# A hybrid attention and delta-rule block: ScalarE copies a pair's open accumulator into a gate's scratch tile, and the last quarter is summed from two tiles

## The chip, the core and the metric

The kernel runs on one core of one Trainium2 chip. The metric is the device time of one execution in microseconds (us). TensorE (PE) multiplies matrices into PSUM, an accumulator memory of banks; VectorE (DVE) and ScalarE (ACT) work element by element on PSUM and on SBUF, the working memory; GpSimd (POOL) does a few small steps; SyncE (SP) issues the transfers. Each engine has an instruction list of its own, which it runs in order, and waits on semaphores for the others.

## The reference

One layer of a hybrid decoder on 16 meta tokens and 512 sequence tokens (528 columns) with a model width of 1024, in float32. Attention and a chunked gated delta rule run side by side on the same normalised input.

```python
hn = rms_norm(h, norm_w)
proj = hn @ w_in                      # widths 1024: aq ak av az dq dk dv dz ..., ga gd
y_a = (o_a * silu(az)) @ w_branch_attn        # o_a: differential attention of aq, ak, av, 8 heads
qkv = silu(causal_depthwise_conv(concat(dq, dk, dv), conv_w))
...
y_d = (o_d * silu(dz)) @ w_branch_delta       # o_d: gated delta rule in chunks of 64, 8 heads
merged = sigmoid(ga) * y_a + sigmoid(gd) * y_d
h = h + merged @ w_out
return rms_norm(h, final_norm_w)[:, N_META:]
```

What counts here is `proj`: each of its blocks is 128 output features x 528 tokens, summed over 1024 inputs.

## The kernel before

**Precision.** Each float32 operand is split into a high and a low part (`wh`, `wl` for weights, `hnH`, `hnL` for the normalised input), and each product is three matmuls: high by high, low by high, high by low (`PASSES`). ACT casts the high part of a weight, DVE subtracts it to get the low one.

**Pairs.** 17 pairs of blocks (`PAIRS`: `ak`, `dk`, `dv`, `dq` blocks with their neighbour) are computed with a Strassen-Winograd scheme: the two blocks by the two halves of the inputs by the two halves of the tokens (`HALF` = 264) form 2x2 block matrices, and seven half-size products replace eight. Each product is 4 input chunks x 3 passes = 12 matmuls with 264 columns. The weights' sums (`wa` to `wd`) are made on DVE while they are split; the tokens' sums lie in `sumH0..3` and `sumL0..3`. The table gives each product its PSUM accumulator, weight, half and part of the tokens, in the order of execution; in a pair `p4` goes to an accumulator `q` of its own:

```python
PRODUCTS = dict(p1=("r", "wa", 0, "b11"), p2=("s", "wa", 1, "b21"), p6=("r", "wb", 1, "t2"), p5=("t", "wb", 0, "t1"),
                p7=("r", "wc", 0, "t3"), p4=("r", "wc", 1, "t4"), p3=("t", "wd", 0, "b22"))
```

The four quarters of a pair (block m, tokens tau) are sums over the products' running sums:

- block 0, first tokens: `r` after p1 (copied by ACT, `snap`) plus `s`
- block 0, second tokens: `r` after p6 (copied by ACT) plus `t` after p3, which p3 adds to p5
- block 1, first tokens: `r` after p7, copied by ACT into the SBUF tile `cn` (`snap_c`), plus `q` (p4)
- block 1, second tokens: `cn` plus `t` after p5, *before* p3 adds to it

The sums are DVE additions of a bank and an SBUF tile (`total`). The third product, p3, is the last of the seven and adds to `t`; so PE waits ahead of it for the event `c+`, which the DVE addition of the last quarter gives when it has read `t`. The sums go to an `xp` tile for `dk`, `dv`, `dq` (a convolution follows) and to a `vT` tile for `ak`, `av`.

**Order.** The program writes every step as a generator that asks for a slot or an event and then for an engine. A planner (`Plan`, lines 95 to 205) gives each engine its next instruction by the earliest estimated time and a rank. The lists are fixed when the program is built: a step that is added or waits for something else makes the planner deal the rest again. Between the matmuls of pairs and single blocks (`product`) stand small products of attention (`ident,e`, `vm,pmT`, `psc<-ak,aq`) and of the delta rule (`S,kT`, `vin,TM`, `u,ktd`, `TM,tds` and the like).

**Slots.** Three weight slots `W`; accumulators from six PSUM banks, at most three for dense products (`pd`); two scratch tiles of a gate, `th` (the two halves of the tile `room3`, 128x512 each), which hold the tanh of a `dz` or `az` block from its ACT instruction until DVE has used it. They become free when the tokens' sums are made.

All instructions go through one helper, so the profile names line 231 for each; rows are told apart by their tiles.

Of the kernel before, what the change touches and what calls it, by code (L numbers as in the profile page):

```python
# [14 lines left out]
ALU = mybir.AluOpType  # L15
# [18 lines left out]
def dense_order():  # L34

    order = []
    for g in range(H // 2):
        k, v, q, z = ([(n, 2 * g), (n, 2 * g + 1)] for n in ("dk", "dv", "dq", "dz"))
        a0, a1 = ([(n, 2 * g + i) for n in ("ak", "av", "aq", "az")] for i in range(2))
        order += k + v + (a0 + q + a1 + z if g else q + a0[2:3] + z[:1] + a0[:2] + a0[3:] + z[1:] + a1)  # L40
    order += [("gd", c) for c in range(KB)] + [("ga", 0)]
    for n in range(KB):
        order += [("ga", n + 1)] * (n < KB - 1) + [(("yd", "ya")[n // 4], 2 * (n % 4) + i) for i in range(2)]
    return order
# [6 lines left out]
                p7=("r", "wc", 0, "t3"), p4=("r", "wc", 1, "t4"), p3=("t", "wd", 0, "b22"))  # L51
# [6 lines left out]
ORDER = dense_order()  # L58
# [3 lines left out]
HALF = L // 2  # L62
# [6 lines left out]
PE, DVE, ACT, POOL, SP = "PE", "DVE", "ACT", "POOL", "SP"  # L69
# [19 lines left out]
class Plan:  # L89
# [24 lines left out]
    def spawn(self, gen, rank=None):  # L114
        time, src = self.here() if self.task else (0.0, SP)
        self.tasks.append(Task(gen, self.task.rank if rank is None else rank, time, src))

    def done(self, event):
        self.events[event] = self.here()
# [146 lines left out]
def hybrid_block(ctx: ExitStack, tc: tile.TileContext, x, meta, wblk, wbd, wout, pcol, prow, out):  # L266
    nc = tc.nc
    plan = Plan({**SLOTS, "wo": 0, "th": 0}, BANKS, ALL_BANKS)
    T, V, A, G, S = (Engine(plan, n, e) for n, e in
                     ((PE, nc.tensor), (DVE, nc.vector), (ACT, nc.scalar), (POOL, nc.gpsimd), (SP, nc.sync)))  # L270
    spawn, done = plan.spawn, plan.done
# [9 lines left out]
    def mk(pl, shape, dt, tag, bufs=None):  # L281
        uid[0] += 1
        kw = {} if bufs is None else {"bufs": bufs}
        return pl.tile(shape, dt, tag=tag, name=f"{tag}_{uid[0]}", **kw)
# [12 lines left out]
    def bank(kind):  # L297

        return mk(ps, [P, 2, 512], F32, kind, SLOTS[kind]) if kind == "psc" else banks_[plan.task.slot]

    def give(kind, at=None):
        plan.give(kind, names_.index(at.tensor.name) if kind in BANKS else 0)
# [9 lines left out]
    def tick(event, n):  # L312
        ticks[event] = ticks.get(event, 0) + 1
        if ticks[event] == n:
            done(event)
        return ticks[event] == n
# [540 lines left out]
    ths = [room[3][:, n, 0:SEQ] for n in range(SLOTS["th"])]  # L857
# [11 lines left out]
    cn = mk(dp, [P, HALF], F32, "cn")  # L869
# [811 lines left out]
    WHOLE = dict(dk=whole_dk, dv=whole_dv, dq=whole_dq, ak=whole_ak, av=whole_av)  # L1681
# [196 lines left out]
    def pair_of_blocks(n):  # L1878

        (n0, i0), (n1, i1) = ORDER[n], ORDER[n + 1]  # L1880
        kind = "xp" if n0 == n1 else "vT"
        acc, to, which = {}, {}, {}
        tokens = slice(0, HALF), slice(HALF, L)

        def take(m):
            if m in which:
                yield f"to {m} {n}"
                return
            which[m] = None
            if kind == "vT":  # L1890
                yield "ap"
            yield (kind,)
            which[m] = plan.task.slot
            to[m] = xps[which[m]][:, 3:3 + L] if kind == "xp" else late["vT"][which[m]]
            done(f"to {m} {n}")

        def snap(key, m, tau):
            yield from take(m)
            yield ACT
            A.copy(out=to[m][:, tokens[tau]], in_=acc["r"])  # L1900
            done(f"{key} {n}")

        def snap_c():
            yield ("cn",)
            yield ACT
            A.copy(out=cn, in_=acc["r"])
            give("pd", acc["r"])
            done(f"c {n}")

        def total(m, tau, of, key, src=None):  # L1910

            yield f"{key} {n}"
            yield from take(m)
            yield DVE
            dst = to[m][:, tokens[tau]]
            V.tensor_tensor(out=dst, in0=acc[of], in1=dst if src is None else src, op=ALU.add)
            if of != "t" or m == 0:
                give("pd", acc[of])
            if of == "t":
                done(f"{key}+ {n}")  # L1920
            if src is not None and tick(f"cn {n}", 2):
                give("cn")
            if tick(f"block {m} {n}", 2):
                name, i = ORDER[n + m]
                spawn(WHOLE[name](i, which[m]), 1)

        follow = dict(p1=lambda: snap("a", 0, 0), p2=lambda: total(0, 0, "s", "a"), p6=lambda: snap("b", 0, 1), p7=snap_c,
                      p4=lambda: total(1, 0, "q", "c", cn), p3=lambda: total(0, 1, "t", "b"))
        for key, (bk, wt, hf, part) in PAIR_PRODUCTS.items():
            if key in ("p6", "p7"):  # L1930
                yield f"{'a' if key == 'p6' else 'b'} {n}"
            if key == "p4":
                spawn(total(1, 1, "t", "c", cn), -1)
            if key == "p3":
                yield f"c+ {n}"
            yield f"{wt} {n}"
            if part in of_sum:
                yield part
            wh, wl, which_w = pairs[n][wt]
            w = wh[:, 512 * hf:512 * hf + 512], wl[:, 512 * hf:512 * hf + 512]  # L1940
            fresh = bk not in acc
            if fresh:
                yield ("pd",)
            for k in range(KB // 2):
                if part in of_sum:
                    x_ = ts_h[of_sum[part]][:, k], ts_l[of_sum[part]][:, k]
                else:
                    x_ = [hn[j][:, k + KB // 2 * (part[1] == "2"), tokens[part[2] == "2"]] for j in range(2)]
                yield PE
                if fresh and k == 0:  # L1950
                    acc[bk] = bank("pd")[:, 0:HALF]
                for m, (a, b) in enumerate(PASSES):
                    T.matmul(acc[bk], w[a][:, k * P:(k + 1) * P], x_[b], start=fresh and k == 0 and m == 0,
                             stop=k == KB // 2 - 1 and m == 2, skip_group_check=not fresh)
            if key in LAST:
                plan.give("W", which_w)
            if key in follow:
                spawn(follow[key](), -1)
        if n == PAIRS[-1]:
            done("sums free")  # L1960
# [33 lines left out]
    def dense():  # L1994
        yield from first_products()
        for n, (name, i) in list(enumerate(ORDER))[2:]:
            if n in PAIRS:
                yield from pair_of_blocks(n)
            elif n not in PAIRED and name not in ("ga", "yd", "ya"):
                yield from product(n)  # L2000
# [244 lines left out]
```

## Time and profile before

| | us |
|---|---|
| median of 3 runs | 752.92 (752.59 to 752.99) |
| profiled execution, its own time | 751.14 |
| span of the profiled execution, first to last instruction | 749.4 |
| TensorE busy | 735.4 (98%) |
| VectorE busy | 629.4 (84%) |
| ScalarE busy | 516.0 (69%) |
| GpSimd busy | 71.8 (10%) |

The span is cut into 40 slices in the page; TensorE is at nine tenths or more in all but the last, and its granted clock is 0.997 on average. 71% of the chain that ended last is TensorE's. In a row of the timeline the first number is the start in us, the second the length drawn; in brackets stands the engine's idle time before the instruction and what ended it. `PEld` is TensorE's loading of the stationary operand, which overlaps its matmuls. In a group's row, `x17 | 6.4, 377` is the count, the total in us and the mean in ns, and after the second bar stand the idle time before such instructions and what ended it.

### The profile page before, as it was taken

To read this page: it belongs to the slowest core of one execution; us is meant where nothing else is said; L and a number is where in the kernel's file an instruction comes from. 1 tells how busy PE (TensorE), PEld (TensorE's weight loads), DVE (VectorE), ACT (ScalarE), POOL (GpSimd) and SP (SyncE) were. 2 spreads that over 40 slices of the span, in tenths; PEclk is the share of its full clock that TensorE was granted. 3 is DMA by queue.
4 is the path that set the end of the run, shared out by engine and by line. 5 is a ranking of instruction groups with operands and counts; after the bars stand their busy time and mean duration, and the time that the engine had idled before them with its cause. 6 is when DMAs were issued, how large, how long until landed. Compare 5 with 4: busy or idle time off the path is not lost.

```text
span 749.4 us, 14381 instructions
## 1 busy us (share of the span) xinstructions
PE 735.4 (98%) x5299; PEld 668.8 (89%) x5299; DVE 629.4 (84%) x1417; ACT 516.0 (69%) x1381; POOL 71.8 (10%) x86
## 2 busy tenths in 40 slices
PE   9999999999999999999999999999999999999996
PEld 7998988899998899998899989888988998899875
DVE  6999999899899889889989898983679879789453
ACT  6369665979974889985597997577785445546132
POOL 2202001202100301300030210000010000000001
PEclk9999999999999999999999999999999999999999
DMA  8130522215232321334032314531122343133602
GB/s 300 59 114 29 142 62 65 70 62 170 62 122 85 73 71 52 120 100 141 29 72 72 120 56 137 212 71 58 57 66 103 142 143 113 54 108 112 231 5 108
DMA packets 45432, 74.34 MB, mean 99 GB/s; under 512 B 20729, under 2 KB 25893, under 8 KB 45362
## 3 DMA queue, kind: packets, MB, share of 16 engines
q1 hardware_dynamic: 45360, 73.43, 30.8%
q8 instruction: 41, 0.67, 0.4%
q14 instruction: 29, 0.24, 0.1%
q10 hardware_dynamic: 2, 0.00, 0.0%
HBM read 67.06 MB, written 6.36 MB: 98 GB/s over the span
## 4 chain that ended last, share of the span: by engine, by line
PE 71%; ACT 12%; DVE 11%; issue 3%; DMA 2%; SPq 0%; POOL 0%; POOLq 0%; DVEq 0%; ACTq 0%
PE bank L231 68%; DVE wl L231 3%; PE psc L231 2%; ACT wh L231 2%; ACT ak L231 1%; ACT TM L231 1%; DMA raw<-in_wblk_dram 1%; DVE tmps L231 1%; DVE ts L231 1%; DMA xt<-in_x_dram 1%; DVE y L231 1%; DVE raw L231 1%; ACT MT L231 1%; DVE ast L231 1%; ACT vr L231 1%
## 5 line engine op out<-in xcount | busy, mean ns | idle before, releaser
L231 PE MATMUL bank<-hnH,wh 128*128 128x512 f32 (+4 forms) x612 | 218.1, 361 | 2.6 <-DVE vT L231 2.1
L231 PE MATMUL bank<-hnL,wh 128*128 128x512 f32 (+4 forms) x612 | 206.1, 342 | 0.0
L231 PE MATMUL bank<-hnH,wl 128*128 128x512 f32 (+4 forms) x612 | 205.8, 342 | 0.0
L231 ACT CAST wh<-raw 128x1024 fp32r<-128x1024 f32 (+1 forms) x123 | 118.0, 960 | 50.7 <-PE bank L231 45.3
L231 DVE TENSOR_TENSOR wl<-raw,wh 128x1024 fp32r<-128x1024 f32 (+1 forms) x123 | 136.8, 1113 | 16.2 <-ACT wh L231 15.8
L231 PEld LDWEIGHTS bank<-hnH,wh 128*128 128x128 f32 x612 | 114.2, 189 | 16.2 <-DVE vT L231 2.8
L231 PEld LDWEIGHTS bank<-hnH,wl 128*128 128x128 f32 x612 | 113.8, 188 | 13.9
L231 PEld LDWEIGHTS bank<-hnL,wh 128*128 128x128 f32 x612 | 114.2, 189 | 10.0
L231 PE MATMUL bank<-sumH,wh 128*128 128x264 f32 x272 | 82.4, 303 | 0.0
L231 PE MATMUL bank<-sumH,wl 128*128 128x264 f32 x272 | 77.2, 284 | 0.0
L231 PE MATMUL bank<-sumL,wh 128*128 128x264 f32 x272 | 77.1, 283 | 0.0
L231 DVE SCALAR_TENSOR_TENSOR y<-xp,pc,y 128x528 f32<-128x528 f32 (+1 forms) x72 | 54.6, 761 | 0.5 <-ACT y L231 0.3
L231 PEld LDWEIGHTS bank<-sumH,wh 128*128 128x128 f32 x272 | 51.5, 189 | 0.6 <-issue 0.2
L231 PEld LDWEIGHTS bank<-sumL,wh 128*128 128x128 f32 x272 | 51.4, 189 | 0.0
L231 PEld LDWEIGHTS bank<-sumH,wl 128*128 128x128 f32 x272 | 51.1, 188 | 0.0
L231 ACT ACTIVATE e<-psc,ast 128x144 f32<-128x144 f32 (+3 forms) x64 | 34.5, 540 | 12.5 <-DVE ast L231 11.4
L231 PE MATMUL bank<-btH,wh 128*128 128x256 f32 x128 | 36.6, 286 | 1.0 <-ACT sn L231 0.9
L231 ACT CAST wh<-st 128x1024 fp32r<-128x1024 f32 x25 | 26.2, 1047 | 15.9 <-PE bank L231 14.6
L231 PE MATMUL bank<-btH,wl 128*128 128x256 f32 x128 | 36.1, 282 | 0.0
L231 PE MATMUL bank<-btL,wh 128*128 128x256 f32 x128 | 36.1, 282 | 0.0
L231 DVE TENSOR_TENSOR wl<-st,wh 128x1024 fp32r<-128x1024 f32 x25 | 30.7, 1229 | 6.2 <-ACT wh L231 6.2
L231 PE MATMUL psc<-ak,aq 128*128 128x264 f32 (+3 forms) x160 | 29.0, 303 | 0.4 <-ACT e L231 0.4
(381 smaller groups left out, 1723.4 us busy)
## 6 DMA issues: line engine op xcount, KB each, us to landing
raw<-in_wblk_dram SPq DMA_DIRECT2D x96, 512.0 KB, 3.5
raw<-in_wout_dram SPq DMA_DIRECT2D x8, 512.0 KB, 4.9
xt<-in_x_dram SPq DMA_DIRECT2D x4, 512.0 KB, 6.6
TM<-gcd SPq DMA_DIRECT2D x8, 256.0 KB, 5.5
xr<-in_x_dram SPq DMA_DIRECT2D x8, 256.0 KB, 6.3
out_dram<-xr SPq DMA_DIRECT2D x7, 256.0 KB, 2.3
room<-scrm SPq DMA_DIRECT2D x12, 128.0 KB, 3.4
oad<-room SPq DMA_DIRECT2D x6, 256.0 KB, 2.0
```

Of the source, the lines that this page charges most:

```text
L231: return real(*args, **kw)
```

## The change

A new step `snap_t` follows the fifth product: it takes a `th` slot, and ACT copies the accumulator `t` (264 columns) into it. The last quarter of a pair is now made by `both`, from the scratch tile and `cn`, so DVE reads two SBUF tiles there and no bank; it then gives the scratch tile back. The third product waits for the copy (event `t`) and no longer for the addition (`c+`). The other three quarters are summed as before; `finished` is the old ending of `total`.

```diff
+        def snap_t():
+            yield ("th",)
+            which["t"] = plan.task.slot
+            yield ACT
+            A.copy(out=ths[which["t"]][:, 0:HALF], in_=acc["t"])
+            done(f"t {n}")
+
+        def both():
+            yield f"t {n}"
+            yield f"c {n}"
+            yield from take(1)
+            yield DVE
+            V.tensor_tensor(out=to[1][:, tokens[1]], in0=ths[which["t"]][:, 0:HALF], in1=cn, op=ALU.add)
+            plan.give("th", which["t"])
+            if tick(f"cn {n}", 2):
+                give("cn")
+            finished(1)
...
         def total(m, tau, of, key, src=None):
...
-            if of != "t" or m == 0:
-                give("pd", acc[of])
-            if of == "t":
-                done(f"{key}+ {n}")
+            give("pd", acc[of])
...
-        follow = dict(p1=lambda: snap("a", 0, 0), p2=lambda: total(0, 0, "s", "a"), p6=lambda: snap("b", 0, 1), p7=snap_c,
+        follow = dict(p1=lambda: snap("a", 0, 0), p2=lambda: total(0, 0, "s", "a"), p6=lambda: snap("b", 0, 1), p5=snap_t, p7=snap_c,
...
             if key == "p4":
-                spawn(total(1, 1, "t", "c", cn), -1)
+                spawn(both(), -1)
             if key == "p3":
-                yield f"c+ {n}"
+                yield f"t {n}"
```

In the built program ACT has 17 more copies, one for each pair, and DVE as many additions as before. PE's matmuls are the same in number and shape. All engines' lists are as before up to the second pair except for the copies and their neighbours; from the third pair on the planner deals the small products differently.

More of the change, by code (lines that the diff above doesn't have):

```diff
@@ L1908, in snap_c, with finished @@
             done(f"c {n}")
+        def snap_t():
[14 more added lines that the diff above has]
+            finished(1)
+        def finished(m):
+            if tick(f"block {m} {n}", 2):
+                name, i = ORDER[n + m]
+                spawn(WHOLE[name](i, which[m]), 1)
         def total(m, tau, of, key, src=None):
@@ L1916, in total @@
             V.tensor_tensor(out=dst, in0=acc[of], in1=dst if src is None else src, op=ALU.add)
-            if of != "t" or m == 0:
-                give("pd", acc[of])
-            if of == "t":
-                done(f"{key}+ {n}")
+            give("pd", acc[of])
             if src is not None and tick(f"cn {n}", 2):
                 give("cn")
-            if tick(f"block {m} {n}", 2):
-                name, i = ORDER[n + m]
-                spawn(WHOLE[name](i, which[m]), 1)
-        follow = dict(p1=lambda: snap("a", 0, 0), p2=lambda: total(0, 0, "s", "a"), p6=lambda: snap("b", 0, 1), p7=snap_c,
+            finished(m)
+        follow = dict(p1=lambda: snap("a", 0, 0), p2=lambda: total(0, 0, "s", "a"), p6=lambda: snap("b", 0, 1), p5=snap_t, p7=snap_c,
                       p4=lambda: total(1, 0, "q", "c", cn), p3=lambda: total(0, 1, "t", "b"))
```

## The prediction

> **What bounds the kernel now.** I read the page's head first, then the busy time by stretch, then who waited for whom on TensorE, and last the rows around the waits.
>
> ```profile
> span 749.4 us, 14381 instructions
> PE 735.4 (98%) x5299; PEld 668.8 (89%) x5299; DVE 629.4 (84%) x1417; ACT 516.0 (69%) x1381; POOL 71.8 (10%) x86
> ```
>
> TensorE (PE) is the bound: it is busy for 735.4 of 749.4 us. Its work does not change (the same 4707 matmuls as the program writes them), so only the 14 us in which it is idle, and what hides inside its busy time, can be won.
>
> ```profile
> core 0: us, PE busy (x) PEld busy (x) DVE busy (x) ACT busy (x) POOL busy (x), PEclk, DMA share, GB/s
> 32.00:135.00 103.00, 101.16 (x705) 92.96 (x703) 96.67 (x225) 74.32 (x191) 12.91 (x12) 1.00 0.30 86
> 135.00:471.00 336.00, 333.01 (x2663) 310.03 (x2663) 304.54 (x718) 279.43 (x831) 42.40 (x41) 1.00 0.29 89
> 471.00:700.00 229.00, 227.95 (x1519) 202.74 (x1520) 184.35 (x368) 135.10 (x306) 5.34 (x6) 1.00 0.33 108
> 700.00:749.40 49.40, 43.17 (x210) 35.75 (x208) 18.56 (x37) 11.56 (x26) 3.30 (x4) 0.99 0.27 95
> ```
>
> The pairs run from 78 to 472 us. From 135 to 471 us PE stands idle for 2.99 us, from 32 to 135 us for 1.84, and the largest idle time, 6.2 us, lies in the last 49 us, which the change does not touch.
>
> ```profile
> PE bank L231 <- DVE vT L231: 2.1, 3, 0.8
> PE bank L231 <- DVE tdmt L231: 0.9, 1, 0.9
> PE bank L231 <- DVE xp L231: 0.2, 1, 0.2
> PEld bank L231 <- DVE vT L231: 2.8, 3, 1.0
> PEld bank L231 <- DVE xp L231: 0.4, 1, 0.4
> ```
>
> The columns are total us, times, longest. The longest line of PE is a wait for VectorE (DVE) writing `vT`, three times; a fourth time it waits for `xp`. `vT` and `xp` are the two kinds of block tile that a pair fills. The four places:
>
> ```profile
> 110.45 0.28 PE L231 MATMUL bank<-sumH,wl 128*128 128x264 f32 x1
> 111.29 0.39 PE L231 MATMUL bank<-hnH,wh 128*128 128x264 f32 x1 [0.55 <-DVE vT L231]
> 111.52 0.28 PE L231 MATMUL bank<-hnL,wh 128*128 128x264 f32 x1
> ...
> 265.03 0.28 PE L231 MATMUL bank<-sumH,wl 128*128 128x264 f32 x1
> 265.52 0.39 PE L231 MATMUL bank<-hnH,wh 128*128 128x264 f32 x1 [0.20 <-DVE xp L231]
> 265.74 0.28 PE L231 MATMUL bank<-hnL,wh 128*128 128x264 f32 x1
> ...
> 345.48 0.28 PE L231 MATMUL bank<-sumH,wl 128*128 128x264 f32 x1
> 346.51 0.39 PE L231 MATMUL bank<-hnH,wh 128*128 128x264 f32 x1 [0.75 <-DVE vT L231]
> 346.74 0.28 PE L231 MATMUL bank<-hnL,wh 128*128 128x264 f32 x1
> ...
> 469.81 0.28 PE L231 MATMUL bank<-sumL,wh 128*128 128x264 f32 x1
> 469.93 0.28 PE L231 MATMUL bank<-sumH,wl 128*128 128x264 f32 x1
> 471.03 0.39 PE L231 MATMUL bank<-hnH,wh 128*128 128x264 f32 x1 [0.82 <-DVE vT L231]
> 471.26 0.28 PE L231 MATMUL bank<-hnL,wh 128*128 128x264 f32 x1
> ```
>
> At each, the fourth product's last matmul (`sumH,wl`) is followed by the third product's first (`hnH,wh`): the spot where the old code waits for `c+`. What it waits for, at the last place, on ScalarE (ACT) and DVE:
>
> ```profile
> 467.27 1.05 ACT L231 CAST wh<-raw 128x1024 fp32r<-128x1024 f32 x1 [1.49 <-PE bank L231]
> 469.07 0.37 ACT L231 COPY cn<-bank 128x264 f32<-128x264 f32 x1
> 469.32 0.50 ACT L231 ACTIVATE e<-psc,ast 128x272 f32<-128x272 f32 x1
> 469.41 1.23 DVE L231 TENSOR_TENSOR wl<-raw,wh 128x1024 fp32r<-128x1024 f32 x1
> 470.55 0.77 DVE L231 TENSOR_TENSOR vT<-bank,cn 128x264 f32<-128x264 f32 x2
> ```
>
> ACT copies `r` into `cn` at 469.07; DVE then still has a weight split of 1.23 us ahead of the sum, starts the sums at 470.55, and PE goes on at 471.03. So the matmuls wait behind a queue, with only the 12 matmuls of the fourth product as cover.
>
> **The change part by part.** *The wait taken away.* Undisturbed matmuls of this shape start 0.12 us apart (469.81 to 469.93). The four gaps are 0.84, 0.49, 1.03 and 1.10 us, so they hold 0.72 + 0.37 + 0.91 + 0.98 = 2.98 us above that spacing. The bracketed idle times add up to 2.32 only; I take the spacing, since a matmul's drawn length (0.28) overlaps the next ones. After each wait the second matmul starts 0.22 to 0.23 us after the first instead of 0.12: 0.11 + 0.10 + 0.11 + 0.11 = 0.43 us more, which I count too. Together -3.4 us; ends -2.3 and -3.4. The weight-load rows, 2.8 + 0.4 = 3.2, lie between.
>
> [...]
>
> *The wait put in.* The third product now waits for ACT's copy of `t`, which follows the fifth product. Behind that stand the seventh and fourth products, 24 matmuls of 0.12 us = 2.9 us.
>
> ```profile
> L231 ACT COPY cn<-bank 128x264 f32<-128x264 f32 x17 | 6.4, 377 | 2.9 <-PE bank L231 2.7
> L231 DVE TENSOR_TENSOR xp<-bank,cn 128x264 f32<-128x264 f32 x18 | 7.6, 428 | 2.9 <-ACT cn L231 2.2 <-PE bank L231 0.6
> L231 DVE TENSOR_TENSOR room<-room,room 128x256 f32<-128x256 f32 x8 | 3.4, 422 | 0.1
> ```
>
> The copy has the shape of the `cn` copy: 0.377 us, of which 0.25 us until ACT takes the next instruction (469.07 to 469.32). 2.9 us of cover leave 2.5, more than any single ACT instruction above. On the path: 0.
>
> *What stands behind the copy on ACT.* At the second pair, where ACT's list has the copy ahead of the weight cast that the same fifth product releases (the rows are the order; `room` is the scratch, `bank_6` holds `t`, `bank_5` holds `r`), before and now:
>
> ```order
> L231 ACTIVATE e_1356,ast_1354<-psc_1363,ast_1354 128x272
> L231 CAST wh_19_117<-raw_16_114 128x1024
> L231 CAST pm_91_717<-e_1290 128x2x16
> L231 COPY cn_167<-bank_5_82 128x264
> L231 CAST pm_92_718<-e_1355 128x2x16
> ```
>
> ```order
> L231 ACTIVATE e_1357,ast_1355<-psc_1364,ast_1355 128x272
> L231 COPY room_33_133<-bank_6_83 128x264
> L231 CAST wh_19_117<-raw_16_114 128x1024
> L231 COPY cn_167<-bank_5_82 128x264
> L231 CAST pm_91_717<-e_1291 128x2x16
> ```
>
> The cast moves 0.25 us back and the `cn` copy moves ahead of a small cast. At the last place of before that cast ran at 467.27 and its split ended at 470.64 (469.41 + 1.23); without the wait the third product would run from 470.05 to 471.5, and only then is the next block needed, so 0.86 us are left and 0.25 fit: 0. If that cover were gone at every pair, 17 x 0.25 = 4.3 us.
>
> *The sum's other source.* DVE reads two SBUF tiles instead of a bank and a tile. The nearest rows are 422 ns for two SBUF tiles with 256 elements and 428 ns with 264 and a bank: the same to 6 ns, 17 x 0.006 = 0.1 us, off PE's path. 0.
>
> *The scratch tiles.* The copy holds one of two, which the gates use too. The row `ACTIVATE room<-bank` shows how little the gates ask of them:
>
> ```profile
> L231 ACT ACTIVATE room<-bank 128x512 f32<-128x512 f32 x18 | 10.8, 599 | 0.2 <-PE bank L231 0.2
> ```
>
> 18 gates in the whole span, and 0.2 us idle before them. 0; at worst a pair waits for one gate's 0.6 us, and that is inside the 2.5 us.
>
> *The new deal.* The planner deals all the work again, and from the third pair on the small products of the chunked delta rule stand elsewhere between the pairs' matmuls. PE at the third pair, around the third product's first rows (`bank_5` holds `t`; `TM,tds` are 32x32 products of the delta rule's inverse), before and now:
>
> ```order
> L231 MATMUL bank_6_83<-tds_1624,TM_744 32x32
> L231 MATMUL bank_6_83<-TM_744,tds_1624 32x32 x8
> L231 MATMUL bank_5_82<-hnH,wh_23_121 128x264
> L231 MATMUL bank_5_82<-hnL,wh_23_121 128x264
> L231 MATMUL bank_5_82<-hnH,wl_24_122 128x264
> ```
>
> ```order
> L231 MATMUL bank_1_78<-vs_1193,pT_1689 128x128 x4
> L231 MATMUL bank_2_79<-sumH_36_136,wh_21_119 128x264
> L231 MATMUL bank_2_79<-sumL_40_140,wh_21_119 128x264
> L231 MATMUL bank_2_79<-sumH_36_136,wl_22_120 128x264
> L231 MATMUL bank_5_82<-hnH,wh_23_121 128x264
> L231 MATMUL bank_5_82<-hnL,wh_23_121 128x264
> L231 MATMUL bank_5_82<-hnH,wl_24_122 128x264
> ```
>
> The small products, which filled the old wait here, now come after the third product and six matmuls of the next block. Everything behind that point is dealt anew, so its waits on chains of small steps are new too, and no row of before shows them. The bounds: PE's idle time from 135 to 471 us outside the waits counted above is 2.99 - 0.20 - 0.75 - 0.82 = 1.22 us, so the gain ends at -1.2. For the loss I take the stretch with the most: from 32 to 135 us it is 1.84 - 0.55 = 1.29 us in 103, which over 336 us would be 4.2, or 3.0 more than now. From 471 to 700 us it is 1.05 us in 229, or 1.5 over 336, 0.3 more. The same planner deals with the same costs, so I stay near the stretch's own 0 and the 0.3, a little above: +0.5.
>
> *Sum*: -3.4 + 0.5 = -2.9 us. The profiled execution took 751.14 us, 1.74 above its span of 749.4, and becomes 748.2. The median of the runs, 752.92, is 1.78 above the profiled execution, which makes 750.0 us, 0.39% faster. I call 0.2% (1.5 us) the least that a measurement tells from no change: faster is below 751.4, slower above 754.4.
>
> **The rivals.** *The new deal eats the gain.* The waits on the delta rule's chains grow by 3.0 instead of 0.5: -0.4, so 752.5 us, no change. For it: `tdmt`, one step of that chain, cost PE 0.9 us in one place. Against it: of the 333 us that PE works there, a chain was late by only 1.2 in all.
>
> *The wait moves to the next weights.* PE reaches the next block up to 1.1 us earlier and finds its split unfinished, because DVE is busy for 304.54 of 336 us. If each of the four gains returned so, nothing would be left: 752.9. At the last place the split ends 0.86 us before it is needed even then, which speaks against it.
>
> *ACT becomes the bound (slower).* Where ACT has no idle time left, each copy delays the small steps of the delta rule behind it, and PE with them.
>
> ```profile
> 160.00:210.00 50.00, 50.00 (x374) 46.99 (x374) 45.12 (x105) 48.34 (x160) 8.10 (x8) 1.00 0.32 96
> ```
>
> In this stretch, with three pairs, ACT is drawn busy for 48.34 of 50 us, 1.66 idle, and gets 3 x 0.377 = 1.13 more. If every copy were paid in full, 17 x 0.377 = 6.4, less 3.4: +3.0, 755.9 us. It decides for slower from 13 of the 17 copies on: (3.4 + 1.5) / 0.377. Against it: from 135 to 471 us ACT is idle for 336 - 279.43 = 56.6 us, and an ACT instruction's drawn length overlaps the next one (0.37 drawn, 0.25 to the next).
>
> [...]
>
> **How the numbers follow.** The forecast as it stands, with the new deal between -1.2 and +1.9: 0.68. The new deal eats the gain: 0.18. The wait moves to the weights: 0.04. ACT becomes the bound: 0.10. So faster 0.68, same 0.22, slower 0.10. The forecast's own range runs from -3.4 - 1.2 = -4.6 (748.3) to -3.4 + 1.9 = -1.5 (751.4). The whole range reaches on to the new deal at its upper bound, 752.5, and leaves out the other two cases and the edges of these.
>
> **What would show it.** Right: no bracketed wait for `vT` or `xp` on PE at the third product; 17 copies `room<-bank` of 128x264 on ACT with about 380 ns each; PE's idle time from 32 to 471 us near 2.5 to 3 instead of 4.8. The new deal shows as new PE waits for ACT or DVE at rows with `S`, `u`, `vin`, `tdmt` or `pmT`. The second rival shows as waits for `wl` or `wh`, the third as ACT without idle time and PE waits for its delta steps, or for `room`. I would be wrong by most if the four waits stood for a DVE that is late in general, so that PE cannot go faster than it anywhere in the pairs.

## The result and the profile after

| | before | after |
|---|---|---|
| median of the runs, us | 752.75 (751.85 to 752.99) | 757.87 (757.69 to 758.22) |
| ratio to before, 95% interval | 1 | 1.0071, 1.0051 to 1.0091 |
| span of the profiled execution, us | 749.4 | 756.1 |

A fourth execution of after took 2721.89 us, a slow one whose cause is not known, and is left out here. The kernel became 0.71% slower, 5.3 us by that ratio; the forecast was 2.9 us faster. The head of the page of after, and its busy time by stretch (the columns are those shown for before):

```profile
span 756.1 us, 14391 instructions
PE 740.0 (98%) x5299; PEld 670.3 (89%) x5299; DVE 630.1 (83%) x1417; ACT 519.7 (69%) x1398; POOL 75.5 (10%) x86
```

```profile
32.00:135.00 103.00, 102.16 (x715) 94.04 (x714) 96.78 (x232) 73.86 (x191) 11.23 (x11) 1.00 0.30 85
135.00:471.00 336.00, 329.82 (x2614) 305.58 (x2613) 297.84 (x697) 277.89 (x835) 46.81 (x42) 0.99 0.27 85
471.00:700.00 229.00, 227.97 (x1533) 202.24 (x1533) 187.01 (x382) 138.55 (x316) 6.31 (x7) 1.00 0.34 107
```

The loss lies from 135 to 471 us, where PE now idles 336 - 329.82 = 6.18 us instead of 2.99. Its mean clock there is 0.99 instead of 1.00. The waits of PE (total us, times, longest), and a third product as an example:

```profile
PE bank L231 <- ACT pT L231: 2.3, 3, 1.1
PE bank L231 <- DVE tdmt L231: 1.5, 2, 0.9
PE bank L231 <- ACT sn L231: 1.4, 3, 0.5
PE bank L231 <- ACT xp L231: 0.9, 1, 0.9
PE psc L231 <- ACT e L231: 0.6, 1, 0.6
```

```profile
112.19 0.28 PE L231 MATMUL bank<-sumH,wl 128*128 128x264 f32 x1
112.31 0.29 PE L231 MATMUL bank<-hnH,wh 128*128 128x264 f32 x1
112.44 0.28 PE L231 MATMUL bank<-hnL,wh 128*128 128x264 f32 x1
```

The lines for `vT` have gone, and here the third product starts 0.12 us after the fourth's last matmul. What is new are waits for ACT. Two of them stand next to each other. PE's rows, ACT's rows at the same time, and PE's busy time and granted clock in stretches of 2 us:

```profile
201.13 0.31 PE L231 MATMUL bank<-ident,pm 128*96 128x128 f32 x1
202.57 0.31 PE L231 MATMUL bank<-ident,pm 128*96 128x128 f32 x1 [1.12 <-ACT pT L231]
203.79 0.39 PE L231 MATMUL bank<-hnH,wh 128*128 128x264 f32 x1 [0.91 <-ACT pT L231]
```

```profile
199.79 1.03 ACT L231 CAST wh<-raw 128x1024 fp32r<-128x1024 f32 x1
200.72 0.35 ACT L231 ACTIVATE MT<-bank,sc 128x128 f32<-128x128 f32 x1
201.10 0.63 ACT L231 CAST ak<-vT 64x528 fp32r<-64x528 f32 x1
201.75 0.38 ACT L231 COPY xp<-bank 128x264 f32<-128x264 f32 x1
202.03 0.48 ACT L231 COPY pT<-bank 128x384 f32<-128x384 f32 x1
202.54 0.59 ACT L231 ACTIVATE aq<-bank 64x512 fp32r<-64x512 f32 x1
203.16 0.59 ACT L231 COPY pT<-bank 128x512 f32<-128x512 f32 x1
```

```profile
202.00:204.00 2.00, 0.52 (x2) 0.33 (x3) 1.94 (x4) 1.93 (x6) 0.00 (x0) 1.00 0.42 66
204.00:206.00 2.00, 2.00 (x15) 2.00 (x14) 0.32 (x2) 1.98 (x5) 0.00 (x0) 0.73 0.75 237
206.00:208.00 2.00, 2.00 (x12) 2.00 (x11) 0.51 (x1) 1.30 (x4) 0.00 (x0) 0.50 0.01 1
208.00:210.00 2.00, 2.00 (x17) 1.98 (x17) 1.03 (x4) 1.36 (x5) 0.00 (x0) 0.92 0.44 119
```

PE transposes `e` at 198.97 and 199.69, but ACT copies the results (`pT`) only at 202.03 and 203.16, behind a weight cast and steps for other tiles. PE is busy for 0.52 of 2 us, and from 204.91 to 208.33 its clock is 0.50.

To compare profiles I use the time from one dense matmul that all kernels have (the 348th of the blocks' products, at 81.83 us in before) to the end of the span, since the start-up differs: that matmul starts between 81.06 and 83.52 us in the profiled executions. From it to the end are 667.57 us before and 672.56 after: +4.99.

There is one profiled execution of each kernel, and one early wait differs between kernels with before's order. VectorE waits for a weight transfer, which takes 4.75 us from issue to landing in before (4.83 in after): 1.28 us in before and 1.98 in the kernel without the wait of the experiments, though the engines' rows of these two start alike up to there, to within 0.1 us. Their rows:

```profile
88.40 0.69 DVE L231 TENSOR_TENSOR st<-raw 128x512 f32<-128x512 f32 x1 [1.28 <-DMA raw<-in_wblk_dram]
...
88.31 0.69 DVE L231 TENSOR_TENSOR st<-raw 128x512 f32<-128x512 f32 x1 [1.98 <-DMA raw<-in_wblk_dram]
```

PE pays for it at 103 us, ahead of the first of the four places: it waits 0.41 us for ACT's `e` in before, 1.10 in the other. So I also give the difference from the dense matmul at 105 us on, behind that wait: +4.9 for after.

### The profile page after: what moved, and what is told of

It is laid out like the page before. It is cut to its first block, busy times and chain, and to the rows that moved or that the text cites. A ratio compares the mean times of both kernels' runs of the same rounds, so it can differ in the third digit from the quotient of the medians.

```text
span 756.1 us, 14391 instructions
## 1 busy us (share of the span) xinstructions
PE 740.0 (98%) x5299; PEld 670.3 (89%) x5299; DVE 630.1 (83%) x1417; ACT 519.7 (69%) x1398; POOL 75.5 (10%) x86
## 4 chain that ended last, share of the span: by engine, by line
PE 74%; ACT 11%; DVE 10%; issue 2%; DMA 1%; POOL 0%; SPq 0%; POOLq 0%; DVEq 0%; ACTq 0%
PE bank L231 72%; DVE wl L231 3%; PE psc L231 3%; ACT wh L231 2%; ACT TM L231 1%; ACT ak L231 1%; ACT MT L231 1%; DVE ast L231 1%; DVE ts L231 1%; DMA raw<-in_wblk_dram 1%; DVE tmps L231 1%; DVE y L231 1%; ACT vr L231 1%; DVE raw L231 1%; ACT e L231 1%
```

## The experiments

My theories were: the loss is in the new deal (A); or in the copies, which make a full ACT late (B); and a part of it is the half clock (C).

**Before's order, with the copies.** The lists are before's row for row, with 17 copies put in where ACT stood at that moment:

```diff
+        def snap_t():
+            yield ACT
+            free = sorted(plan.slots["th"])
+            if free:
+                tn.append(ths[free[-1][2]][:, 0:HALF])
+                nc.scalar.copy(out=tn[0], in_=acc["t"])
...
-            V.tensor_tensor(out=dst, in0=acc[of], in1=dst if src is None else src, op=ALU.add)
+            V.tensor_tensor(out=dst, in0=tn[0] if tn and of == "t" and m else acc[of], in1=dst if src is None else src, op=ALU.add)
```

> The instruction lists of the kernel before, row for row on PE, DVE, POOL and SP; the 17 ACT copies of t are added where ACT is first free, and the last quarter is summed from the scratch tile, so that the third product waits for the copy alone. The planner is told nothing of the copies, so nothing is dealt anew. Theory A (the new deal lost the time, the copies cost nothing): the four waits go and nothing else moves, 752.8 - 3.4 = 749.4 us (748.9 to 750.2). Theory B (the copies make a full ACT late, and PE with it): the waits go, but the copies are paid, 753 us or more, with PE waiting for ACT between 160 and 210 us.

Measured: ratio 1.0031 (1.0016 to 1.0046), from the common matmul to the end +2.3 us, from 105 us on +1.8. The change without its deal is still slower, as theory B had it, though PE is busy for 49.90 of the 50 us from 160 to 210 us, where B expected its waits. Matmul by matmul, the third products start earlier by 3.7 us in all (the four waits, their restarts and three small restarts), and some 5.5 us come back elsewhere.

**The copies alone.** The same, but the sum reads the bank as before, and p3 waits for it:

> As the run above, but the copies are made and not used: the last quarter is summed from the bank as before, and the third product still waits for that sum. This is the price of 17 ACT copies alone in the old deal. Theory A: 752.8 us, within 0.5. Theory B: 755 to 757 us, up to 17 x 0.25 = 4.3 us more than before.

Measured: 1.0044 (1.0029 to 1.0059), +2.9 us, from 105 us on +2.8, as theory B had it. The dearest place is one copy; ACT's rows there, and PE's:

```profile
455.20 0.59 ACT L231 ACTIVATE room<-bank 128x512 f32<-128x512 f32 x1
...
456.49 0.99 ACT L231 ACTIVATE ao<-ao,ass 128x128 f32<-128x128 f32 x3
458.43 0.38 ACT L1935 COPY room<-bank 128x264 f32<-128x264 f32 x1 [0.95 <-DVE room L231]
458.70 1.05 ACT L231 CAST wh<-raw 128x1024 fp32r<-128x1024 f32 x1
459.65 0.40 ACT L231 ACTIVATE ao<-ao,ass 128x128 f32<-128x128 f32 x1
```

```profile
460.11 0.33 PE L231 MATMUL bank<-ident,ao 128*128 128x128 f32 x1 [0.77 <-ACT ao L231]
```

The copy waits 0.95 us for the scratch tile, in which a gate's tanh of 455.20 still lies. Behind it on ACT stand a cast and the `ao` for which PE waits: 0.94 us more there than before. This wait comes from the way the copies are put in here: the planner knows nothing of them and gives them no slot. In the changed kernel, where it does, the copies never wait for a scratch tile:

```profile
L231 ACT COPY room<-bank 128x264 f32<-128x264 f32 x17 | 6.4, 375 | 1.2 <-PE bank L231 1.1
```

At other places the copy just takes ACT's time ahead of a delta step (`u,ktd`, +0.25 and +0.23 us).

**The new deal alone.** After's lists without the 17 copies:

```diff
-            A.copy(out=ths[which["t"]][:, 0:HALF], in_=acc["t"])
+            plan.spend(ACT, A.time("copy", (), dict(out=ths[which["t"]][:, 0:HALF], in_=acc["t"])))
```

> The lists of the changed kernel without the 17 copies (the last quarter is summed from the scratch tile as it stands, so that quarter's values are not the reference's). Theory A: the time stays at 757 to 758.3 us, with PE's waits near 201 to 204 us still there. Theory B: without the copies ACT is on time, 752 to 753.5 us.

Measured: 1.0056 (1.0040 to 1.0073), +3.5 us, from 105 us on +3.7: most of the loss, as theory A had it. The `pT` wait is as long as with the copies, so it belongs to the deal, and the mean clock from 135 to 471 us is 0.99 here too:

```profile
PE bank L231 <- ACT pT L231: 2.2, 3, 1.1
```

**The idle time filled.** After, with 12 and 9 transposes repeated in the two idle times at 201 us, so that PE is not idle for long there:

```diff
+            if h == 1 and i == 3:
+                for n in (0, 1, 2, 3) * 3:
+                    nc.tensor.transpose(pt[:, n * P:(n + 1) * P], es[0][:, chunk(n)], ident)
...
+            if h == 1 and i == 2:
+                for _ in range(9):
+                    nc.tensor.transpose(po[0:96, P:2 * P], pm.rearrange("p a t -> p (a t)").bitcast(F32), ident)
```

> The changed kernel with 12 + 9 repeated 128-column transposes on PE that fill its two idle times between 201 and 204 us (they write the same values again; about 2.3 us of work where PE has 2.0 us of idle time). Theory C (after those idle times PE's clock was granted at half for 3.4 us, which costs 1.7 us): the clock stays at 1.00 there and the time falls to 756.3 us. If the half clock does not follow from the idle time: 758.0 us, with the half clock still there.

Measured: 1.0052 (1.0038 to 1.0066), +3.6 us, 1.4 less than after (1.2 from 105 us on; the intervals of the two ratios overlap, so this size rests on the profiles). The clock stays at 1.00, as theory C had it:

```profile
200.00:210.00 10.00, 9.12 (x79) 8.87 (x78) 5.74 (x10) 8.76 (x22) 0.00 (x0) 1.00 0.37 104
```

**The wait alone.** Before's lists, no copies, and p3 waits for nothing (the line with the copy is taken out of the first experiment):

> Before's lists row for row, no copies; the last quarter is added from the scratch tile as it stands, so its values are left out, and the third product waits for nothing. It measures what the wait is worth by itself. Theory D (the wait only moves: what PE wins at the four places it loses again at the next thing that DVE or ACT has late): the net gain is that between the two kernels with copies, 0.6 us, so about 751.6 against 752.2. Theory E (the wait is worth its 3.7 us, and what came back in the kernel with copies came back because of the copies): 748.5. Between them 750 would say half and half.

Measured: 0.9990 (0.9979 to 1.0000), 751.6 against 752.0, at the edge of no change; -0.3 us from the common matmul on, -1.0 from 105 us on. The waits with their restarts are worth 3.7 gross and some 1 net, though no copy is in the way. Two of them stand again a few rows later, and a third in part at a product that waits for ACT:

```profile
267.92 0.33 PE L231 MATMUL bank<-ident,ao 128*128 128x128 f32 x1 [0.27 <-ACT ao L231]
...
346.90 1.16 PE L231 MATMUL bank<-qT,kT 128*128 128x128 f32 x8 [0.38 <-DVE qT L231]
...
471.15 1.16 PE L231 MATMUL bank<-qT,kT 128*128 128x128 f32 x8 [0.44 <-DVE qT L231]
```

Before's engines in the stretches around the four places, which the prediction did not use (the third busy time is DVE's, the fourth ACT's):

```profile
103.00:119.00 16.00, 15.03 (x96) 13.67 (x96) 15.90 (x45) 6.54 (x16) 0.00 (x0) 1.00 0.41 132
258.00:274.00 16.00, 15.80 (x201) 14.36 (x200) 12.12 (x25) 14.60 (x40) 1.15 (x2) 1.00 0.20 66
340.00:357.00 17.00, 16.25 (x112) 14.86 (x110) 17.00 (x48) 8.44 (x21) 0.00 (x0) 1.00 0.49 156
466.00:482.00 16.00, 15.18 (x99) 13.63 (x99) 16.00 (x43) 8.16 (x20) 0.00 (x0) 1.00 0.69 247
```

What PE wins at each place (the wait and its restart) and what it has lost again 6 to 14 us later, matmul by matmul against before:

| place | won, us | lost again, us | kept, us |
|---|---|---|---|
| 111 us | 0.82 | 0.32 | 0.50 |
| 265 us | 0.46 | 0.46 | 0.00 |
| 346 us | 1.03 | 0.72 | 0.30 |
| 471 us | 1.08 | 0.94 | 0.14 |

At the last two places, the dearest, DVE has no idle time at all: PE goes at DVE's pace, and most of a wait taken away at one product comes back at the next that needs DVE. The first two show that DVE's busy time is not the whole rule: at 111 us DVE is nearly as full and most is kept, and at 265 us DVE has 3.88 us idle and all is lost, behind ACT, which has 1.40.

**Copies in four pairs.** Before's lists, copies only where PE waited:

```diff
-            if free:
+            if free and PAIRS.index(n) in (1, 7, 11, 16):
```

> Before's lists with copies in only the four pairs where PE waited (at 111, 265, 346 and 471 us); the last quarter is read from the copy there and from the bank elsewhere. If a copy costs the same everywhere, four cost 4/17 of 2.9 = 0.7 us. Theory D: -0.6 + 0.7, no change, 752.3. Theory E: -3.7 + 0.7 = -3.0, 749.2, better than both kernels. A third way: the copy costs only where ACT is late (457, 158, 284, 396 us, none of the four pairs), then 0.7 falls away and the result is that of the kernel without copies.

Measured: 0.9989 (0.9979 to 0.9999), -1.1 us, from 105 us on -0.9. These four copies cost nothing that shows, and win as little as no wait at all; place by place they keep what the kernel above keeps, to within 0.1 us. The third way of the expectation holds.

**Copies but three.** The same line with `not in (3, 8, 15)`:

> Before's lists with copies in 14 pairs: left out in those whose copies run at 156, 283 and 458 us, where the kernel with all 17 in before's order lost 0.24, 0.23 and 0.94 us. If a copy costs by its place, because of what stands behind it on ACT there, those 1.4 us come back: 753.6 becomes 752.2. If a copy costs the same in each pair (2.9 / 17 = 0.17), only 0.5 comes back: 753.1.

Measured: 0.9995 (0.9983 to 1.0007), +1.2 us where all 17 had +2.3; from 105 us on +0.4 against +1.8. At the three places PE gets back 0.32, 0.23 and 0.94 us, the last being the wait for the scratch. So a copy costs by its place: leaving out 3 of 17 gave back half of the 2.8 us by the profiles, and 2.7 by the ratios (1.0031 to 0.9995). Both are more than the 0.5 of equal prices; how much more, the runs do not settle.

**Is DVE's order or its load to blame?** First I moved the split of 1.22 us behind `qT` at the two places, on the four-copies kernel:

```diff
+BEHIND = (741, 1012)        # rows of DVE's list: held until qT, four rows on, is issued
```

> The kernel with four copies, and in VectorE's list, at the two places before the products of qT with kT (348 and 472 us), the weight split of 1.22 us stands behind qT instead of ahead of the sums; nothing else moves. If the wait for the sums only moved to qT because DVE comes to both late, PE now gets through: the two qT waits (0.54 + 0.10 and 0.58 + 0.10 us above the spacing) go, -1.3 us, so about 750.3 where the kernel with four copies had 751.6 and before 752.0. If the split itself is then late, PE waits for wl at the next block and the time stays at 751.6. If the wait is worth nothing in any place because the next engine is always late, also 751.6.

Measured: 1.0018 (1.0005 to 1.0032), +2.1 us. PE's waits for `qT`, by total, times and longest:

```profile
PE bank L235 <- DVE qT L240: 3.4, 2, 1.8
```

These are not the two waits aimed at, which went (0.51 and 0.58 us less), but those at the next `qT`. It does not test what it should: held so long, the split reads a weight tile that already belongs to a later block (the values of those blocks are left out) and waits for that block's transfer. DVE then idles for 0.68 and 1.13 us:

```profile
348.70 1.23 DVE L238 TENSOR_TENSOR wl<-raw,wh 128x1024 fp32r<-128x1024 f32 x1 [0.68 <-DMA raw<-in_wblk_dram]
...
474.75 1.23 DVE L238 TENSOR_TENSOR wl<-raw,wh 128x1024 fp32r<-128x1024 f32 x1 [1.13 <-DMA raw<-in_wblk_dram]
```

So I left the split and moved `qT` itself ahead of the sums:

```diff
+AHEAD = (742, 1013)         # rows of DVE's list: from here qT, three rows on, goes first
```

> The kernel with four copies, and in VectorE's list, at the two places before the products of qT with kT, the row that makes qT stands right behind the weight split and ahead of the two sums of vT and a step of the inverse (0.83 us earlier); the split stays where it was, and nothing else moves. If the wait moved to qT only because DVE took the sums first, the two qT waits (0.54 + 0.10 and 0.58 + 0.10 us above the spacing) go: 1.3 us less than with the four copies alone, about 750.3 to 750.7 where before has 752.0 to 752.6, a ratio near 0.9975. If DVE is late in general there, the sums come 0.7 us later and hold up what waits for them (vT's transposes, the accumulator's release, the next qT at 355 and 480 us): the ratio stays at 0.999.

Measured: 0.9990 (0.9981 to 0.9999), as the four copies alone. The two waits are gone (0.54 + 0.10 and 0.58 + 0.10 us), and stand again at the next `qT`, 0.71 and 0.80 us longer than they were:

```profile
356.44 1.16 PE L236 MATMUL bank<-qT,kT 128*128 128x128 f32 x8 [0.55 <-DVE qT L236]
...
481.66 1.16 PE L236 MATMUL bank<-qT,kT 128*128 128x128 f32 x8 [0.78 <-DVE qT L236]
```

At these two places it is DVE's load, then, and not the order in which it takes these rows. This was a reason I named for being most wrong, and did not price.

**Other deals.** Before's steps, with no copy, and one constant of the planner (its hand-over time from an engine) changed by 10 ns:

```diff
-    HOP = {PE: 200, DVE: 130, ACT: 140, POOL: 90, SP: 0}
+    HOP = {PE: 200, DVE: 130, ACT: 150, POOL: 90, SP: 0}     # the others: DVE 140; PE 210; POOL 100
```

> Before's steps, no copies; the planner's constant for a hand-over from ACT is 150 ns instead of 140, which changes nothing but the deal. If any new deal costs what the changed kernel's deal cost without its copies (+3.5 us), 755 to 756. If a deal is as good as another and that one was unlucky in its place at 201 us, within 1 us of 752.2. If before's deal is merely the best of many, between: 753 to 755, with new PE waits of 0.3 to 1 us for ACT and DVE in other places.

> Before's steps, no copies; the planner's constant for a hand-over from DVE is 140 ns instead of 130. As in the kernel with ACT's constant: 755 to 756 if any new deal costs 3.5 us, within 1 us of 752.2 if deals are alike. Two such deals give a first idea of the spread: if they lie over 2 us apart, the new deal of the changed kernel is one draw of a wide lot.

> Before's steps, no copies, PE's hand-over constant 210 ns instead of 200. The two deals so far cost +5.2 and +2.4 us. If before's deal is a favourable one among many, this too is slower, by 1 to 6 us: 753 to 758. If deals are alike within 1 us, 751 to 753; faster than before would say that before's deal is an ordinary one and the changed kernel drew badly.

> Before's steps, no copies, POOL's hand-over constant 100 ns instead of 90; POOL does few steps, so that fewer rows move than with the other constants (about 600 on ACT against 1770). If the loss comes with the amount that is dealt anew, it is smaller than with the others: 752 to 754. If one displaced chain is enough, 753 to 758.

| constant | ratio, 95% interval | common matmul to the end |
|---|---|---|
| ACT 150 | 1.0068, 1.0049 to 1.0086 | +5.5 us |
| DVE 140 | 1.0034, 1.0020 to 1.0047 | +1.8 us |
| PE 210 | 1.0079, 1.0066 to 1.0092 | +6.4 us |
| POOL 100 | 0.9978, 0.9966 to 0.9991 | -1.2 us |

Deals of the same steps lie 1% apart, 7.6 us by the profiles. The changed kernel's deal without copies (1.0056) lies among them. ACT's constant gives even the same kind of place, with another releaser; stretches of 2 us again, and PE's wait:

```profile
202.00:204.00 2.00, 0.00 (x0) 0.00 (x1) 1.90 (x4) 1.95 (x7) 0.00 (x0) 1.00 0.26 57
206.00:208.00 2.00, 2.00 (x11) 1.99 (x11) 1.09 (x3) 0.47 (x2) 0.00 (x0) 0.50 0.59 225
```

```profile
204.00 0.39 PE L231 MATMUL bank<-hnH,wh 128*128 128x264 f32 x1 [2.17 <-DVE vrm L231]
```

The deal with POOL's constant is faster than both kernels of this case, without the change: 751.09 us against 752.62. It is also the one that deals least anew: PE's rows are before's up to 425 us, where those of the other three part from before's at 60 to 87 us. I did not run more deals, so how often one of this kind wins stays open.

## Why the prediction was wrong

Counted from 105 us on, the +4.9 us come apart so: the wait, net, -1.0 (the wait alone); the new deal 3.7 + 1.0 = +4.7 (the deal alone, less that); the copies in the new deal 4.9 - 3.7 = +1.2. The timed ratios give -0.8, +5.0 and +1.1, but the intervals of the kernels with and without copies overlap, so this last term rests on the profiles and on the runs in before's order. Counted from the common matmul at 81.83 us, with the early wait in them, the three are -0.3, +3.8 and +1.5.

- *The wait taken away, -3.4:* right in gross, 3.7 by the matmuls, and wrong as a term of the sum: net it was -1.0 by the profile and -0.8 by the ratio. The first step that failed is taking what PE waits as what PE gains. I had set 304.54 of 336 us of DVE against it as an average, and only for the next block's weights; in the stretches of the two longest waits DVE was at 17.00 of 17 and 16.00 of 16, and the next row that needs it is `qT`, right behind the third product.
- *The wait put in, 0:* right. No third product of after waits for its copy.
- *What stands behind the copy on ACT, 0:* wrong. With all 17 copies in before's order it was +2.8 (1.8 + 1.0, and 2.8 with the copies alone), of which 0.94 is the wait for a scratch tile that the change itself does not have; in the new deal it was +1.2. The bound that I had worked out and dropped was 4.3. I had tested one place, the last, and there the copy did turn out free; about half of the cost sat in three others.
- *The scratch tiles, 0, at worst 0.6 "inside the 2.5 us":* the 0 was right: no copy of after waits for a scratch tile, and the gates' idle time is 0.2 us as before. The reason for the bound was wrong. The slack of 2.5 us covers p3; it does not cover what ACT has queued behind a copy that waits. Where a copy did wait, in before's order, 0.95 us cost PE 0.94.
- *The sum's other source, 0:* right: 426 to 428 ns for two SBUF tiles, 424 to 428 with a bank. The rows of `vT`:

```profile
L231 DVE TENSOR_TENSOR vT<-room,cn 128x264 f32<-128x264 f32 x8 | 3.4, 426 | 0.0
L231 DVE TENSOR_TENSOR vT<-bank,cn 128x264 f32<-128x264 f32 x8 | 3.4, 424 | 0.0
```

- *The new deal, +0.5 between -1.2 and +3.0:* the term most mis-sized, +4.7. "The same planner deals with the same costs, so I stay near the stretch's own 0" was the faulty step, and the one that cost most: four deals of the same steps lie from -1.2 to +6.4 us. The bounds came from before's own stretches, and these show one deal, not the spread of deals; nor could they hold the 3.42 us at half clock. The one place at 201 us makes 2.0 us of idle time and 1.2 to 1.4 of half clock; the rest was not placed wait by wait. Why the planner's estimates go wrong there was not tried.
- *The rivals.* "The new deal eats the gain" names the largest part, at two thirds of its size (3.0 against 4.7), and looked for it at the delta rule's chains, where the largest waits came at attention's `pT`. "The wait moves to the next weights" had the right idea and the wrong row: at the two dearest places it moved to `qT`. "ACT becomes the bound" ended on the right side for another reason: the stretch it named, 160 to 210 us, is where after lost most, but the deal without copies has the same waits there.

## What to carry to other kernels

A wait of the bound engine is worth only what the engines it needs next can give back: ask for their busy time in the few us around the wait, of all of them and not only of the one it waits for, and where one has no idle time, count on little (here 1.0 of 3.7 us was kept). A small instruction on an engine that is idle 17% of a stretch can still cost PE more than its length, if it waits for a slot and something urgent is queued behind it (here a copy of 0.38 us cost 0.94). Where a list scheduler deals everything anew, first measure how far two deals of the unchanged steps lie apart (here 1%), and judge a change with the old order held.

## What the runs showed of the hardware

In after the granted clock fell to half behind a short, incomplete lull. PE was busy for 1.43 of the 3.41 us from 201.50 us on, and then ran for 3.42 us at 0.50; behind that, from 208.33 to 208.50 us, the clock was 1.00 again:

```profile
201.50:204.91 3.41, 1.43 (x10) 1.24 (x11) 2.58 (x4) 3.31 (x7) 0.00 (x0) 1.00 0.50 140
204.91:208.33 3.42, 3.42 (x18) 3.42 (x17) 0.69 (x1) 2.70 (x9) 0.00 (x0) 0.50 0.19 38
```

Two idle times of 1.12 and 0.91 us so cost 1.2 to 1.4 us more than themselves, and with transposes that nobody needs in their place the clock was 1.00 from 200 to 210 us. Three waits that stood alone were followed by 1.00 for at least 8 us: 0.94 us, up to 135.31, in before, 0.92, up to 136.57, and 0.90, up to 458.42, in after. With ACT's constant a single one of 2.17 us was followed by 0.50 from 206 to 208 us. What decides whether the clock halves was not shown.
